# Delta rule: five second orientations of the inverse by TensorE transposes instead of second fp32 products

## The chip, the core and the metric

The kernel runs on one core of a Trainium2 chip, as one program. The metric is device microseconds of one execution; the runs are given as a median with the lowest and the highest. A core has TensorE for matrix products (results land in PSUM, eight banks of which this kernel names 4 "acc", 2 "mm" and 2 "tr"), VectorE, ScalarE and GpSimd for elementwise work, and SyncE, whose queue starts most DMAs. Every engine takes its own instructions in order; one that needs another engine's result waits on a semaphore.

## The reference, cut to what matters

A first stack of two layers works on 256 latent tokens (and 256 of context), a second stack of two layers on the 256 tokens alone. A layer of the second stack is FFN, mixer, FFN, each behind a norm. The mixer runs a gated delta rule with 8 heads beside a dilated attention with 12; both are merged by gates. The delta rule is worked out in chunks, and within a chunk a triangular system is solved:

```python
    m = jnp.where(strict, jnp.einsum('nbhid,nbhjd->nbhij', kb, kc) * decay, 0.0)
    a = m + jnp.eye(C, dtype=f32)
    u_c = lax.linalg.triangular_solve(a, vb, left_side=True, lower=True, unit_diagonal=True)
    w_c = lax.linalg.triangular_solve(a, kb * jnp.exp(gc)[..., None], left_side=True,
                                      lower=True, unit_diagonal=True)
    def step(state, xs):
        v_new = u_i - jnp.einsum('bhcd,bhde->bhce', w_i, state)
        o_i = (jnp.einsum('bhcd,bhde->bhce', q_i * jnp.exp(g_i)[..., None], state)
               + jnp.einsum('bhij,bhje->bhie', qk_i, v_new))
```

## The kernel before

All large products are done in two float32r parts of each factor, as three products of 128x128 by 256 columns (`mm3`: ah by w_hi, al by w_hi, ah by w_lo); the delta rule's small products are in fp32. Weight tiles come through `w_raw`, are split by ScalarE (`w_hi`) and VectorE (`w_lo`), up to three tiles ahead of their use.

The mixer is the class `Hybrid`. Its `inner` runs, one after the other, the products with `w_in` (23 groups of 256 columns after the first pairs), those of gate b, those with `w_b`, those of gate a, those with `w_a` and those with `w_o`. Beside them go "sides", generators that `pump` steps between two blocks of a product: `chains` (the heads of the delta rule), `convolve`, the dilated attention, the vectors of the conditions. Every instruction, whatever emits it, passes through `Engine.call`, so the profile shows line 75 for nearly all; the rows below are told apart by tiles.

`chains` holds up to four heads active (NB = 4). Each head is a generator, `delta`, whose steps end at a `yield`; a step is emitted when `Times`, a table of estimated costs, says that its inputs are ready. A head may start when its query, key and value have been convolved, and the places for queries and keys hold six heads. So the order of the work is fixed when the program is built, by the estimates, and on the chip each engine follows it in order.

`delta` treats two chunks of 128 tokens together (`for c in range(2)`), so a step has two products or a multiple. It first builds `MQ`, the masked products of the keys. Then it inverts 1 + M. `X` is the inverse and `XT` its transpose; both lie in one tile, `XX` (d_XX in the rows). `MT` is M's transpose within one level of blocks (`level`, made by GpSimd). Blocks of 8 come first, by squares, then four levels of 16, 32, 64 and 128 in the loop `for i in range(1, 5)`, in each a product lv by X into `t1` and one of t1 by XT, subtracted from XT. Each level needs X and XT, and before the change each of the pair is made by an fp32 product of its own into one half of a PSUM bank. After the inverse follow, each a step with one or two products: the new values (vb), the outputs and the state S (kd and MQ), the second chunk's (S with k and q, then S with XX, then MQ), a norm of the head's outputs (ScalarE's squares, GpSimd's power, VectorE's scaling), and two transposes of the output, after which the head is done.

Where the products of gate a end, a loop waits for the heads, with every step emitted at once whether or not its inputs are ready by the estimates:

```python
        while not chain.done:
            progress()
```

Only then do the products with `w_a` follow, which need all heads' outputs.

Of the kernel before, what the change touches and what calls it, by code (L numbers as in the profile page):

```python
# [28 lines left out]
class Times:  # L29
    """Estimates of the times at which the engines end what they have been given; by these the instructions of  # L30
    independent parts are put in order."""
# [33 lines left out]
class Engine:  # L65
    """An engine whose instructions' times are estimated as they are emitted."""
# [37 lines left out]
class Timed:  # L104
    """The engines, with estimates of their times."""
# [7 lines left out]
class Side:  # L113
    """Work emitted beside TensorE's products: without a rate, as it can go on; else up to rate steps per us of
    these, while what engine has been given ends within spare us."""
# [33 lines left out]
class Weights:  # L149
    """Weight tiles in the order of their use: loaded ahead, then split in two float32r parts."""  # L150
# [8 lines left out]
    def add(self, ap, offset, row, k, c):  # L159
        """A tile of k blocks of 128 rows by c columns, the first at offset, rows row apart."""  # L160
        self.plan.append((dview(ap, offset, [[row, 128], [128 * row, k], [1, c]]), k, c))
        return len(self.plan) - 1

    def up(self, wg, go, wu, uo, row, f0, f1, lead):
        """Pairs of the gate's and the other factor's columns; with lead, the tiles of the first two alternate."""
# [47 lines left out]
class Build:  # L213
    def __init__(self, nc, tc, I, out, es):
# [10 lines left out]
        # the residual stream, transposed; a second one (the context's); the modulated input in two parts  # L225
# [3 lines left out]
        # besides, for the products begun before a norm's statistics are known: its input * A, and B  # L229
# [9 lines left out]
    def ring(self, pool, shape, dtype, name, bufs):  # L239
        """A tile; its memory's last use counts in the times."""  # L240
        p, t = pool.tile(shape, dtype, name=name, bufs=bufs), self.times
        old = self.rings.setdefault(name, [])
        old.append(p)
        if len(old) > bufs:
            p0 = old.pop(0)
            t.note(t.read, p, max(t.when(x, p0) for x in (t.read, t.written)))
        return p

    def free(self, name, bufs):
        """The time at which the next of a ring's tiles is free."""  # L250
# [3 lines left out]
    def pipeline(self, n, stages, may=lambda i: True, begun=None):  # L254
        """The stages of n items, each when what it needs is done; later items' go in between. A stage: a function
        of the item, one that names its bank, and (s, m) if it may be at most m items before stage s."""
# [27 lines left out]
    def timed(self, gen):  # L284
        """Steps of gen, each when what the last one emitted will be done."""
# [13 lines left out]
    def bank(self, many):  # L299
        """A bank for a product's output; many: those for accumulation besides."""  # L300
# [15 lines left out]
    def rsqrt(self, dst, src, mul, add):  # L316
        """dst = (src * mul + add) ** -0.5"""
# [15 lines left out]
    def forced(self, f):  # L333
        """f(), in which nothing is waited for."""
# [4 lines left out]
    def run(self, gen):  # L339
        """gen yields where other work may go between its products."""  # L340
        for _ in gen:
            self.pump()

# [1 line left out]
    def load_consts(self):  # L345
        """What the first modulation needs."""
# [58 lines left out]
    def aln(self, i, j):  # L405
        """ALPHA * the norm's factors and shifts."""
# [9 lines left out]
    def ada_src(self, name):  # L416
        """name: (stack, layer, index)"""
# [5 lines left out]
    def ada_gen(self, pool, jobs):  # L423
        """The vectors of the conditions, on VectorE: weights times the condition's column, block after
        block; their sums over the partitions end with TensorE and wait in self.pending for that."""
# [44 lines left out]
    def partial(self, dst, t, acc):  # L470
        """Sums over the 32 partitions of a quarter: column 32 b + j of acc to partition j of the quarter, column b."""
# [3 lines left out]
    def reduce_one(self):  # L475
        """The sums over the quarters; those of columns 128 v + 32 c + j go to partition 32 c + j, column v."""
# [10 lines left out]
    def fill(self, n):  # L487
        """Work for TensorE while it would wait."""
# [14 lines left out]
    def mod_cols(self, shift, scale, g=None, b=None, mul=1.0):  # L503
        """Columns A, B of x * (1 + scale) + shift with x = n * g * mul + b."""
# [19 lines left out]
    def gemm_b(self, pairs, rhs, n, evac, ks=8, lead=False, tail=False, many=False, norm=None):  # L524
        """Outputs [128 columns, n tokens]; pairs: lists of the tiles (over k) of 256 columns.
        evac(first block, number of blocks, [128, blocks, 256]) for 256 tokens, evac(block, [128, 512]) for 512.
        lead: the first two pairs go together, block of k by block of k, as rhs comes; with a norm, begun before it,
        and evac has to add a column per block, its last argument.
        tail: the last pair's blocks come one by one. many: see bank()."""
# [35 lines left out]
    def gemm_early(self, pairs, norm, evac):  # L565
        """The first two pairs' products of a norm's input * A and of B; meanwhile the norm is done."""
# [47 lines left out]
    def gemm_a2(self, tiles, lhs, evac):  # L614
        """Outputs [128 tokens, 2 token tiles, 256 columns], in one bank; tiles over k."""
# [14 lines left out]
    def gemm_a(self, tiles, lhs, toks, evac, tags="acc", groups=1, middle=None):  # L630
        """Outputs [128 tokens, c columns] for each token tile; tiles over k. With groups > 1, all tiles for
        the first group of token tiles, then all for the next; middle: called amid the first group's."""
# [4 lines left out]
        for g in range(groups):  # L637
            ts = range(g * toks // groups, (g + 1) * toks // groups)
            kk = 0
            for n, ti in enumerate(tiles):  # L640
                if 0 < g == groups - 1:
                    # the tiles before this one are no longer needed
# [22 lines left out]
def norm_mem(tile):  # L665
    """Memory of a norm; tile(name, shape)"""
# [5 lines left out]
class Norm:  # L672
    """A norm over the features of h [128, 8, tokens], features in the partitions, for one or more streams
    (h, memory): the sums are gathered as blocks of 128 features come; then norm * A + B in two float32r parts.
    For a layer norm h is shifted by the mean of its first 256 features, which keeps the variance's differences
    small."""

    def __init__(self, b, kind, streams=None, slow=True):
        """slow: the blocks come slowly enough for GpSimd to add up the first ones."""
# [6 lines left out]
    def early(self, A, B):  # L686
        """The products with norm * A + B begin before the statistics are known."""
# [4 lines left out]
    def blocks(self, i, k, n):  # L692
        """Blocks k .. k + n - 1 of stream i have come."""
# [51 lines left out]
    def sums(self, i, keep=0):  # L745
        """The sums over the features, per token, but for the last blocks."""
# [13 lines left out]
    def stats(self, i=0):  # L760
        """Per token 1 / std, and -mean / std for a layer norm."""
# [13 lines left out]
    def spread(self, i):  # L775
        """The statistics in every partition, [128, tokens], in PSUM."""
# [6 lines left out]
    def finish(self):  # L783
        """The statistics of the first stream; while they come TensorE sums up vectors of the conditions."""
# [6 lines left out]
    def apply(self, hi, lo, A, B, i=0, each=None, middle=None):  # L791
        """hi, lo [128, 8, 256] of norm * A + B; for a layer norm h becomes the plain norm."""
# [62 lines left out]
def residual(b, gate, norm):  # L855
    """h += gate * product, block by block, and the next norm's sums."""
# [6 lines left out]
class Layer0:  # L863
    """Retention and FFN of the first layer: latents and context together (512 tokens)."""
# [3 lines left out]
    def __init__(self, b):  # L868
# [9 lines left out]
        for h in range(4):  # L878
# [3 lines left out]
            else:  # L882
                # they go together
# [39 lines left out]
    def residual(self, gates, norms):  # L923
        """evac(block, [128, 512]) of products."""
# [9 lines left out]
    def inputs(self, es):  # L934
        """The inputs, transposed and modulated by the first two vectors of the conditions, whose columns come 256
# [1307 lines left out]
```

## Time and profile before

| | |
|---|---|
| median of 3 runs | 2923.53 us (2921.91 to 2925.88) |
| span of the profiled execution, from its first instruction to its last | 2918.0 us |
| own time of the profiled execution beside its span | not given apart; the runs' median is 5.5 us above the span |
| TensorE busy | 2821.7 us, 97% |
| VectorE busy | 2106.7 us, 72% |
| ScalarE busy | 1308.9 us, 45% |
| GpSimd busy | 282.0 us, 10% |
| mean granted clock of TensorE | 0.978 |

Matmuls are pipelined and their ends are modelled, so the busy time of TensorE counts overlapping instructions' latency once and does not say how dense they are; the start of one and of the next do. "PEld" is TensorE's load of the stationary factor, shown apart. An fp32 product leaves two records in the trace, a transpose one. In a row of waits, the name behind the arrow is what came last. Times in timelines are us from the span's start.

### The profile page before, as it was taken

Reading aid. Unit: us, or ns where it says so; the run is one execution under the profiler, and the core shown is the slowest. Engines: PE = TensorE matmul, PEld = TensorE weight load, DVE = VectorE, ACT = ScalarE, POOL = GpSimd, SP = SyncE. Lnnn points to the kernel's source line nnn. Section 1 sums busy time; section 2 is a strip of 40 time slices with the busy share of each in tenths; the row PEclk is TensorE's granted clock in tenths of the full one; section 3 lists DMA queues with packets and bytes.
Section 4 is the critical chain, followed back from the end, with each engine's and each line's share of the span. In section 5 each row is a group of like instructions: output and inputs, shape, how many; then the busy total and the mean of one; then the engine's idle time right before and its main releaser. Section 6 shows DMA issues by size and latency. Waiting matters only on the chain.

```text
span 2918.0 us, 49485 instructions
## 1 busy us (share of the span) xinstructions
PE 2821.7 (97%) x19509; PEld 2591.5 (89%) x19509; DVE 2106.7 (72%) x3405; ACT 1308.9 (45%) x2229; POOL 282.0 (10%) x359
## 2 busy tenths in 40 slices
PE   8999998999999998998999999999999999999999
PEld 5878887888877788998999988999999998999999
DVE  6888887887877665787777777777565577666654
ACT  4433324322225444444445655444444466654543
POOL 0000002000010000001002223110010022130100
PEclk9999998999999998998999999999999999999999
DMA  6444441666654352875876523457556663224564
GB/s 236 146 145 136 142 149 55 220 224 218 233 181 141 99 136 94 265 257 173 276 259 201 148 84 113 142 184 228 185 169 184 186 179 116 80 76 151 166 185 132
DMA packets 432221, 488.36 MB, mean 167 GB/s; under 512 B 34650, under 2 KB 362300, under 8 KB 431988
## 3 DMA queue, kind: packets, MB, share of 16 engines
q1 hardware_dynamic: 430948, 484.59, 53.2%
q8 instruction: 153, 2.51, 0.4%
q10 hardware_dynamic: 1040, 0.60, 0.1%
q14 instruction: 80, 0.66, 0.1%
HBM read 484.07 MB, written 1.05 MB: 166 GB/s over the span
## 4 chain that ended last, share of the span: by engine, by line
PE 46%; DVE 4%; ACT 2%; issue 1%; POOL 1%; DMA 0%; DVEq 0%; ACTq 0%; POOLq 0%
PE ps_acc L75 24%; PE ps_mm L75 21%; DVE w_lo L75 1%; PE ps_tr L75 1%; ACT w_hi L75 1%; DVE n_t L75 1%; DVE al L75 0%; DVE n_a L75 0%; POOL d_t L75 0%; ACT n_a L75 0%; DVE d_XX L75 0%; DVE da_st L75 0%; POOL d_MT L75 0%; DVE ada_acc L75 0%; ACT d_t L75 0%
## 5 line engine op out<-in xcount | busy, mean ns | idle before, releaser
L75 DVE TENSOR_TENSOR w_lo<-w_raw,w_hi 128x1024 fp32r<-128x1024 f32 (+2 forms) x676 | 818.5, 1221 | 432.8 <-ACT w_hi L75 429.1
L75 ACT ACTIVATE w_hi<-w_raw 128x1024 fp32r<-128x1024 f32 (+2 forms) x686 | 700.6, 1030 | 505.5 <-PE ps_acc L75 226.2
L75 PE MATMUL ps_mm<-ah,w_hi 128*128 128x256 f32 (+2 forms) x2272 | 697.5, 307 | 15.2 <-ACT w_hi L75 7.7
L75 PE MATMUL ps_mm<-ah,w_lo 128*128 128x256 f32 (+2 forms) x2272 | 677.5, 298 | 2.2 <-DVE w_lo L75 2.2
L75 PE MATMUL ps_mm<-al,w_hi 128*128 128x256 f32 (+2 forms) x2272 | 678.6, 299 | 0.4
L75 PEld LDWEIGHTS ps_mm<-ah,w_hi 128*128 128x128 f32 (+1 forms) x2272 | 433.1, 191 | 39.8 <-issue 12.6
L75 PEld LDWEIGHTS ps_mm<-ah,w_lo 128*128 128x128 f32 (+1 forms) x2272 | 433.7, 191 | 16.9 <-DVE w_lo L75 3.2
L75 PEld LDWEIGHTS ps_mm<-al,w_hi 128*128 128x128 f32 (+1 forms) x2272 | 433.1, 191 | 12.9 <-DVE al L75 1.4
L75 PE MATMUL ps_acc<-ah,w_hi 128*128 128x256 f32 (+2 forms) x1456 | 436.9, 300 | 1.2 <-ACT ah L75 1.2
L75 PE MATMUL ps_acc<-al,w_hi 128*128 128x256 f32 (+2 forms) x1456 | 436.4, 300 | 0.4 <-DVE al L75 0.4
L75 PE MATMUL ps_acc<-ah,w_lo 128*128 128x256 f32 (+2 forms) x1456 | 435.5, 299 | 0.2 <-DVE w_lo L75 0.2
L75 DVE SCALAR_TENSOR_TENSOR ada_acc<-ada_w,cact,ada_acc 128x512 f32<-128x512 f32 x476 | 353.7, 757 | 14.9 <-DMA ada_w<-ada_w 10.2
L75 PEld LDWEIGHTS ps_acc<-ah,w_hi 128*128 128x128 f32 x1456 | 275.5, 189 | 11.3 <-ACT ah L75 1.6
L75 PEld LDWEIGHTS ps_acc<-ah,w_lo 128*128 128x128 f32 x1456 | 276.3, 190 | 10.4 <-DVE w_lo L75 0.7
L75 PEld LDWEIGHTS ps_acc<-al,w_hi 128*128 128x128 f32 x1456 | 275.6, 189 | 10.5 <-DVE al L75 0.7
L75 PE MATMUL ps_acc<-hh,w_hi 128*128 128x256 f32 (+1 forms) x800 | 237.0, 296 | 0.0
L75 PE MATMUL ps_acc<-hl,w_hi 128*128 128x256 f32 (+1 forms) x800 | 236.7, 296 | 0.0
L75 PE MATMUL ps_acc<-hh,w_lo 128*128 128x256 f32 (+1 forms) x800 | 236.6, 296 | 0.0
L75 POOL TENSOR_TENSOR n_a<-n_a 128x512 f32<-128x512 f32 (+1 forms) x28 | 40.4, 1443 | 1352.9 <-ACT n_a L75 1187.5
L75 PEld LDWEIGHTS ps_acc<-hh,w_lo 128*128 128x128 f32 x800 | 150.9, 189 | 4.4
L75 PEld LDWEIGHTS ps_acc<-hh,w_hi 128*128 128x128 f32 x800 | 150.9, 189 | 4.4
L75 PEld LDWEIGHTS ps_acc<-hl,w_hi 128*128 128x128 f32 x800 | 150.9, 189 | 4.4
(386 smaller groups left out, 4555.0 us busy)
## 6 DMA issues: line engine op xcount, KB each, us to landing
ada_w<-ada_w SPq DMA_DIRECT2D x448, 256.0 KB
w_raw<-w_in SPq DMA_DIRECT2D x132, 512.0 KB
w_raw<-ffn_w SPq DMA_DIRECT2D x128, 512.0 KB
w_raw<-ffn_wg SPq DMA_DIRECT2D x88, 512.0 KB
w_raw<-ffn_wu SPq DMA_DIRECT2D x88, 512.0 KB
w_raw<-ffn_wd SPq DMA_DIRECT2D x80, 512.0 KB
w_raw<-ret_w_in SPq DMA_DIRECT2D x48, 512.0 KB
w_raw<-na_w_qkv SPq DMA_DIRECT2D x24, 512.0 KB
```

Of the source, the lines that this page charges most:

```text
L75: r = f(*args, **kw)
```

## The change

Five times in a head, the second orientation of a matrix is no longer made by a second product in the same step. A new helper, `turned(dst, src)`, transposes both chunks of src on TensorE into a fresh bank and has ScalarE copy them to dst. It is used for MT (the square of M, from t1, where VectorE copied the second product's half before), for X after the square of the inverse, and for X after the first three levels of the loop. (The transposes into X at the start only move into the helper.) Each use is a step of its own, with a `yield` ahead of it. The subtraction in the loop works on XT alone, 256 columns in place of 512.

```diff
...
+        def turned(dst, src):
+
+            ps = bank()
+            for c in range(2):
+                tr(ps[:, cs[c]], src[:, c, :], ident)
+            act(dst, two(ps), AF.Copy)
+
         level(MT, 0)
         yield
         tt(out=XT, in0=eye, in1=MT, op=OP.subtract)
         yield
-        ps = bank()
-        for c in range(2):
-            tr(ps[:, cs[c]], MT[:, c, :], ident)
-        act(X, two(ps), AF.Copy)
+        turned(X, MT)
         yield
         ps = bank()
         for c in range(2):
             mm(ps[:, cs[c]], MT[:, c, :], X[:, c, :], start=True, stop=True)
-            mm(ps[:, 256 + 128 * c:384 + 128 * c], X[:, c, :], MT[:, c, :], start=True, stop=True)
         act(t1, two(ps), AF.Copy)
-        nc.vector.tensor_copy(MT, two(ps[:, 256:512]))
+        yield
+        turned(MT, t1)
         yield
...
         ps = bank()
         for c in range(2):
             mm(ps[:, cs[c]], X[:, c, :], XT[:, c, :], start=True, stop=True)
-            mm(ps[:, 256 + 128 * c:384 + 128 * c], XT[:, c, :], X[:, c, :], start=True, stop=True)
-        act(XX, both(ps), AF.Copy)
+        act(XT, two(ps), AF.Copy)
+        yield
+        turned(X, XT)
         yield
...
                 mm(ps[:, cs[c]], t1[:, c, :], XT[:, c, :], start=True, stop=True)
-                if i < 4:
-                    mm(ps[:, 256 + 128 * c:384 + 128 * c], XT[:, c, :], t1[:, c, :], start=True, stop=True)
+            tt(out=XT, in0=XT, in1=two(ps), op=OP.subtract)
+            yield
             if i < 4:
-                tt(out=XX, in0=XX, in1=both(ps), op=OP.subtract)
-            else:
-                tt(out=XT, in0=XT, in1=two(ps), op=OP.subtract)
-            yield
+                turned(X, XT)
+                yield
```

As the order of emission follows the estimates, it changes from the first head on. On ScalarE in the first layer, where the first head's square of M is copied, there stands now one copy more:

```order
 L75 ACTIVATE da_k<-ps_mm 128x512
 L75 ACTIVATE d_v<-n_t 128x256
+L75 ACTIVATE d_MT<-ps_acc 128x256
 L75 ACTIVATE w_hi<-w_raw 128x1024
 L75 ACTIVATE n_a<-n_a,da_st 128x128
```

The copy into MT has moved to ScalarE, between a value's convolution and a weight tile's split; VectorE's copy of the same matrix is gone from its own queue.

On TensorE in the second layer, where the last two heads end (tiles with their numbers; ident_76 by d_MT is the transposing of a head's output, d_S by d_XX the second chunk's new values, ps_mm rows are the products of gate a), the kernel before has:

```order
L75 MATMUL ps_acc_27018<-d_S_26883,d_XX_26284 128x128
L75 MATMUL ps_acc_27021<-ident_76,d_MT_26302 128x128 x2
L75 MATMUL ps_mm_26987<-ah_68,w_hi_26892 128x256
L75 MATMUL ps_mm_26987<-al_69,w_hi_26892 128x256
L75 MATMUL ps_mm_26987<-ah_68,w_lo_26893 128x256
```

At the corresponding place of the changed kernel (behind the last product of gate a; ps_mm_27344 is the first product with w_a) stands:

```order
L75 MATMUL ps_acc_27289<-d_XX_26679,d_MT_26787 128x128 x2
L75 MATMUL ps_acc_27295<-ident_76,d_MT_26563 128x128 x2
L75 MATMUL ps_acc_27299<-d_XX_26679,d_t1_26678 128x128 x2
L75 MATMUL ps_acc_27304<-d_vb_26785,d_XX_26679 128x128
L75 MATMUL ps_acc_27307<-d_t1_26678,d_kd_26786 128x128
L75 MATMUL ps_acc_27307<-d_t1_26678,d_MQ_26939 128x128
L75 MATMUL ps_acc_27312<-d_S_27303,d_k_26473 128x128
L75 MATMUL ps_acc_27312<-d_S_27303,d_q_26251 128x128
L75 MATMUL ps_acc_27317<-d_S_27303,d_XX_26679 128x128
L75 MATMUL ps_acc_27320<-d_t1_26678,d_MQ_26939 128x128
L75 MATMUL ps_acc_27332<-ident_76,d_MT_26787 128x128 x2
L75 MATMUL ps_mm_27344<-ah_68,w_hi_26972 128x256
```

Before, products of gate a stand between the last heads' steps, and 54 of them behind the last head's transposes; now the last head's steps stand next to each other, from the loop that waits for the heads, and the products with w_a directly behind.

## Rows read from the trace of the kernel before

**Rows 1.** The page's part 1: busy us, share of the span, instructions.
```profile
PE 2821.7 (97%) x19509; PEld 2591.5 (89%) x19509; DVE 2106.7 (72%) x3405; ACT 1308.9 (45%) x2229; POOL 282.0 (10%) x359
```

**Rows 2.** Each engine's busy us by windows: delta stage, first layer, then second.
```profile
1680.00:1720.00 40.00, 34.84 (x272) 32.33 (x271) 29.23 (x77) 23.73 (x57) 5.30 (x9) 0.96 0.24 68
...
2600.00:2640.00 40.00, 39.91 (x348) 39.53 (x347) 24.48 (x54) 17.69 (x50) 12.53 (x18) 1.00 0.28 80
```

**Rows 3.** TensorE's waits (us, times, longest): first layer; last row: second.
```profile
PE ps_acc L75 <- ACT d_t L75: 6.9, 4, 4.2
...
PE ps_acc L75 <- POOL d_t L75: 2.4, 2, 2.2
PE ps_acc L75 <- ACT d_XX L75: 2.0, 2, 1.3
PE ps_acc L75 <- DVE d_XX L75: 0.9, 2, 0.6
...
PE ps_acc L75 <- POOL d_t L75: 1.1, 2, 0.9
```

**Rows 4.** TensorE's timeline at four fp32 products: start, duration, operands.
```profile
1641.95 0.39 PE L75 MATMUL ps_acc<-d_XX,d_MT 128*128 128x128 f32 x2
...
1642.96 0.28 PE L75 MATMUL ps_mm<-al,w_hi 128*128 128x256 f32 x1
1643.08 0.29 PE L75 MATMUL ps_mm<-ah,w_lo 128*128 128x256 f32 x1
```

**Rows 5.** The same timeline at two transposes.
```profile
1636.56 0.38 PE L75 MATMUL ps_acc<-ident,d_MT 128*128 128x128 f32 x2
...
1636.90 0.28 PE L75 MATMUL ps_mm<-al,w_hi 128*128 128x256 f32 x1
```

**Rows 6.** Tile view of XX: count, ns min/median/max, first, last start.
```profile
L75 PE MATMUL ps_acc<-d_t,d_XX x192: 275/275/421, 1670.0 to 2634.8; 128*128 128x128 f32 x192
...
L75 PE MATMUL ps_acc<-d_XX x128: 270/275/348, 1652.5 to 2620.1; 128*128 128x128 f32 x128
L75 DVE TENSOR_TENSOR d_XX<-d_XX,ps_acc x80: 404/678/690, 1649.3 to 2638.4; 128x512 f32<-128x512 f32 x48, 128x256 f32<-128x256 f32 x32
...
L75 PE MATMUL ps_acc<-d_MT,d_XX x64: 275/275/275, 1642.2 to 2614.7; 128*128 128x128 f32 x64
```

**Rows 7.** Timeline of weight loads, the second layer's last head.
```profile
2636.45 0.52 PEld L75 LDWEIGHTS ps_acc<-d_XX,d_MT 128*128 128x128 f32 x4
...
2637.69 0.52 PEld L75 LDWEIGHTS ps_acc<-d_XX,d_t 128*128 128x128 f32 x4 [0.28 <-ACT d_t L75]
...
2638.92 0.30 PEld L75 LDWEIGHTS ps_acc<-d_vb,d_XX 128*128 128x128 f32 x2
...
2639.84 0.31 PEld L75 LDWEIGHTS ps_acc<-d_t,d_MQ 128*128 128x128 f32 x2
```

**Rows 8.** ScalarE's timeline at the same place.
```profile
2637.26 0.38 ACT L75 ACTIVATE d_t<-ps_acc 128x256 f32<-128x256 f32 x1 [1.04 <-PE ps_acc L75]
```

**Rows 9.** VectorE's timeline, the same head's last steps.
```profile
2638.44 0.42 DVE L75 TENSOR_TENSOR d_XX<-d_XX,ps_acc 128x256 f32<-128x256 f32 x1 [0.45 <-PE ps_acc L75]
...
2652.39 0.28 DVE L75 TENSOR_TENSOR d_MT<-d_MT,ps_acc 128x128 f32<-128x128 f32 x1
...
2656.77 0.47 DVE L75 TENSOR_SCALAR d_MT<-d_MT,d_st 128x128 f32<-128x128 f32 x2
```

**Rows 10.** GpSimd's timeline, the same head's norm.
```profile
2654.23 0.95 POOL L75 TENSOR_TENSOR d_st<-d_st,mhalf 128x2 f32<-128x2 f32 x1
```

**Rows 11.** TensorE's busy us and granted clock by windows, first layer.
```profile
1685.00:1690.00 5.00, 1.61 (x14) 1.00 0.01 2
1690.00:1695.00 5.00, 4.19 (x21) 0.66 0.37 110
```

**Rows 12.** TensorE's timeline: the product that ends the first window's wait.
```profile
1690.81 0.49 PE L75 MATMUL ps_acc<-d_k 128*128 128x128 f32 x2 [4.21 <-ACT d_t L75]
```

More of the change, by code (lines that the diff above doesn't have):

```diff
@@ L1974, in delta @@
         yield
-        def both(ps):
-            return ps.rearrange("p (a c n) -> p a c n", a=2, c=2)
         ps = bank()
```

## The prediction

> **What bounds the kernel now.** I read the page first. TensorE is busy for 97% of the span, VectorE for 72%, ScalarE for 45% [rows 1]. A busy TensorE is not always a useful one, so the windows over the two mixers come next: in the second layer's delta stage 39.91 of 40 us are busy, and the worst window of the first layer's still has 34.84 [rows 2]. The waits of TensorE in these stages say what the rest is. In the first layer 6.9 us end with ScalarE's copies into t1, 2.4 with GpSimd's scaled mask, 2.0 and 0.9 with copies and subtractions into XX, 12.2 us together; in the second the longest such group is 1.1 us [rows 3]. So TensorE's own instruction stream is the limit in this part of the program: the delta rule is laid between the large products, its hand-offs hide behind them, and a microsecond of TensorE work removed there is a microsecond off the end, as long as products remain to hide the hand-offs.
>
> **What the swap saves.** One fp32 product of 128x128 takes two TensorE passes: four of them, the first at 1641.95, run until the next product's pace is reached, (1642.96 - 0.12 - 1641.95) / 4 = 0.2225 us each, 0.12 us being the pitch of the large products [rows 4]. Two transposes run from 1636.56 to 1636.90 - 0.12, so 0.11 us each [rows 5]. Each swap is worth 0.1125 us of TensorE. The counts come from the tile view, at two records for a product [rows 6]: 192 / 2 = 96 products t1 by XX in the loop, 64 / 2 = 32 with MT as the stationary side, and half of the 128 / 2 = 64 squares of X, which is 32. All of these 160 become transposes: 160 x 0.1125 = 18.0 us saved, 9.0 us in each layer.
>
> The Trainium skill (FP8 and Floating Point Precision, TensorE Precision Notes) counts four passes of the array for a true fp32 product. Were a transpose a single pass of the four, the ratio would be 4 to 1, the saving 160 x 0.167 = 26.7 us instead of 18.0, and the forecast below would come out 8.7 us lower. The rows show 2 to 1, and the rows decide; I give it no chance of its own.
>
> **What it adds off TensorE.** A product that came out of the same bank as its twin now has to wait for that twin's copy, be transposed and be copied again: 5 more steps in each head's chain, 35 in place of 30, 80 over 16 heads. Engine time is no problem by itself. ScalarE gets five more 256-column copies a head at 0.38 us [rows 8], 1.9 us a head and 30 us over both layers at most (its one 512-column copy gets shorter), on an engine busy for 23.7 of 40 us [rows 2]. VectorE's three subtractions fall from 0.68 us [rows 6] to 0.42 [rows 9]. None of this is on TensorE's path while products cover it.
>
> **The cover runs out.** Here the order decides. Before, the last transposes of a layer's last head stand 78 (first layer) and 54 (second layer) product rows ahead of the end of the gate's products, 9 and 6 us at 0.12 us each. With five steps more per head, and head 4 starting only when head 0 has left its buffers, the heads are not done when the gate's products end. The loop ahead of the products with w_a then emits all that is left at once, with nothing in between: 36 TensorE instructions in the first layer, 47 in the second, counted in the order of the change. In this tail TensorE waits for each hand-off.
>
> The price of a hand-off is read where the last head ran almost alone, from the load of one step's weights to that of the next [rows 7]. A pair of products and ScalarE's copy: 2636.45 to 2637.69, 1.24 us, the copy starting at 2637.26 [rows 8]. A pair and VectorE's subtraction: to 2638.92, 1.23 us. A single product and a copy of 128 columns: to 2639.84, 0.92 us. A turn (two transposes and a copy) is in no row as such; I take the pair's step less 2 x 0.11, 1.02 us. The head's last stretch is a product (0.58 us to its result), the norm from VectorE's addition at 2652.39 [rows 9] to GpSimd's power ending at 2654.23 + 0.95 [rows 10], then 0.47 us of scaling [rows 9] and 0.05 us for each of two hand-offs: 3.9 us before the last transposes can go.
>
> Second layer: the last head has still to go through 9 pair steps (11.1), 3 turns (3.1), 2 single ones (1.8) and the last stretch (3.9), with 0.4 of transposes and a product ahead and 0.2 behind: 20.6 us. In the same rows stand 33 products and 14 transposes, 33 x 0.22 + 14 x 0.11 = 8.9 us of work that has to be done anyway. Idle: 11.7 us. First layer: 6 pair steps (7.4), 1 turn (1.0), 2 single ones (1.8), the last stretch (3.9) and 0.7 at the ends: 14.8 us, less 26 products and 10 transposes, 6.9 us. Idle: 7.9 us. Together 19.6 us. From below I bound this by 16 us, if the second head in the tail and the engines' queues overlap a sixth better than the steps alone; from above by 24 us, if a weight split of about 1 us stands ahead of a copy on ScalarE or VectorE a few times.
>
> **Two smaller terms.** Hand-offs that do stand between products cost TensorE (12.2 + 1.1) / 480 = 0.03 us a step before [rows 3]; 80 more steps add 2 us. Bounds: nothing, or a stall as that at 1690.81, where TensorE stood 4.21 us [rows 12], once more. Then the clock. That stall left 1.61 us busy in five, and the next five ran at a mean granted clock of 0.66, a stretch at 1.2 GHz in place of 2.4, 0.34 x 5 = 1.7 us lost [rows 11]. Each tail ends in a head alone, whose pair steps keep TensorE at work for under half the time, and in 3 us of nothing. I expect one such stretch at least in each: 3.4 us from below if it falls, 6.8 if two do; I take 4.
>
> **Sum.** -18.0 + 19.6 + 2 + 4 = +7.6 us. The profiled execution's span is 2918.0 us, which becomes 2925.6. The profile gives no other time of that execution; the median of the runs lies 5.5 us above the span, so I carry the difference over: 2923.5 + 7.6 = 2931.1 us, 0.26% slower. A measurement of this kernel can tell about 0.2%, 5.8 us.
>
> **Rivals.**
> (a) The clock holds in the tails. For it: a tail is not empty, two heads overlap in most of it. Against it: [rows 11]. It gives 2923.5 - 18.0 + 19.6 + 2 = 2927.1, no change to be told.
> (b) Faster: the new interleaving loses the first layer's own stalls, the 12.2 us of [rows 3], with them the 1.7 us of slow clock behind the longest, and adds no new ones, so that the 2 us fall away too: 2931.1 - 15.9 = 2915.2. VectorE's shorter subtractions and the spread of the heads over more products speak for it; against it, the longest ended with a copy on ScalarE [rows 12], which gets more of these. It decides from 13.4 us on, nearly all of the 15.9, since the forecast has to fall from 7.6 us above the old time to 5.8 below it.
> (c) ScalarE comes late in the middle: two more stalls of 4.2 us, each with its 1.7 us of clock: 2931.1 + 11.8 = 2942.9. For it: in-order copies, 30 us more of them. Against: 23.7 of 40 us busy.
> (d) Transposes lower the clock among the products. One slow stretch for each of 16 heads, 16 x 1.7 = 27 us: 2958. Against it: beside the transposes at 1636.56 the products keep their 0.12 us pitch [rows 4, 5]. The Trainium skill (TensorE: Matmul & The Clock Gate, Part 4: PE-mode transpose) says that a transpose does not count as a busy TensorE in the way that a product does; by that rule more transposes mean more slow stretches, and the trace bears it out nowhere that products stand on both sides.
>
> **Chances.** The forecast 0.50, (a) 0.27, (b) 0.08, (c) 0.12, (d) 0.03. The forecast's own range is 2926 to 2938. A third of it lies within 0.2% of 2923.5, so: slower 0.34 + 0.15 = 0.49, the same 0.16 + 0.27 = 0.43, faster 0.08. The range for 8 in 10 runs from 2921 (the tails at their lower bound, clock unharmed) to 2942, leaving out most of (b) and (d) and half of (c).
>
> **What would show it.** In the changed profile: TensorE's delta instructions as 160 fewer products, 0.11 us each for the transposes; waits of TensorE for XX, t1 and S copies of some 8 and 12 us in the last 15 to 21 us ahead of w_a's products, where before there were none; the granted clock at a half there or right behind; layers otherwise as before. Wrong are: the steps, if the tails measure under 14 us idle in all; the clock term, if it stays at 1.00 through both; the whole, if the waits ahead of the tails change by more than 6 us either way.

## The result, and the profile after

| | before | after |
|---|---|---|
| median | 2922.72 us (2920.82 to 2925.88, 4 runs) | 2939.6 us (2934.06 to 2943.99, 4 runs) |
| ratio | | 1.0054 [1.0041, 1.0066] |
| span of the profiled execution | 2918.0 us | 2932.3 us |
| mean granted clock of TensorE | 0.978 | 0.973 |

The changed kernel is 16.9 us slower by the medians, 12 to 19 by the interval of the ratio. The forecast said 7.6 us slower, in a range of 2921 to 2942: the sign and the range hold, but the forecast size is less than half of the measured one.

The page's part 1 of the changed kernel, which answers to [rows 1]:

```profile
PE 2820.6 (96%) x19349; PEld 2585.8 (88%) x19349; DVE 2095.8 (71%) x3389; ACT 1326.5 (45%) x2309; POOL 293.2 (10%) x359
```

160 TensorE instructions are gone, two for each product becoming one for each transpose; ScalarE has 80 more. Rows of the tile view of XX show 128 of the 160 transposes (the other 32 turn t1), beside [rows 6] (count, ns min/median/max, first and last start):

```profile
L75 PE MATMUL ps_acc<-ident,d_XX x128: 270/272/477, 1658.9 to 2664.6; 128*128 128x128 f32 x128
L75 ACT ACTIVATE d_XX<-ps_acc x112: 357/383/407, 1596.8 to 2664.9; 128x256 f32<-128x256 f32 x112
L75 DVE TENSOR_TENSOR d_XX<-d_XX,ps_acc x80: 402/415/423, 1647.3 to 2667.4; 128x256 f32<-128x256 f32 x80
```

The windows that answer to [rows 2], one of the first and one of the second layer's delta stage (busy us of PE, PEld, DVE, ACT and POOL, then TensorE's clock), and the longest waits of TensorE in the first layer, which answer to [rows 3]:

```profile
1680.00:1720.00 40.00, 35.12 (x261) 32.73 (x260) 28.25 (x75) 23.70 (x59) 5.71 (x10) 0.91 0.30 86
2600.00:2640.00 40.00, 39.17 (x334) 38.39 (x333) 24.70 (x53) 23.68 (x68) 19.98 (x24) 1.00 0.28 87
```

```profile
PE ps_acc L75 <- DVE d_MT L75: 5.3, 5, 2.4
PE ps_acc L75 <- DVE d_MQ L75: 3.9, 2, 2.6
...
PE ps_acc L75 <- ACT d_t L75: 1.0, 3, 0.4
```

The copies into t1 (d_t in the rows) on which TensorE waited for 6.9 us now hold it for 1.0. VectorE's MQ has come in their place, and its work on a head's outputs, which lie in MT's tile by then; of the 5.3 us on these, 2.9 belong to the end of the layer, the tail below. The second layer's window at 2600 is full as before, so the loss is not here.

To place the time I matched the large products (those with w_hi or w_lo, the same in every kernel) of two traces by number. Between the 6000th, ahead of the first mixer of the second stack, and the 12000th, between the two mixers, the changed kernel gains 1.2 us on the kernel before; from there to the last it loses 17.4. These are called the layers' lags below, -1.2 and 17.4. Ahead of the 6000th, where the programs are alike, traces lie -1.9 to 10.2 us from before's, so a lag places a difference better than a median does. Each lag is that of one traced execution. Where other runs repeat a layer's instructions, one by one, the second layer's lag comes again within 0.1 us (17.3), and layers left as before give lags of 0.3 us at most; but the changed first layer gives -1.2, 3.3 and -0.2 in three traces, so a first-layer lag is known to some 4 us only.

The second layer's lag has two places. The first is in the middle of the stage. TensorE's busy time and granted clock (the column behind POOL's) by windows, changed kernel, then the kernel before:

```profile
2585.00:2590.00 5.00, 1.74 (x13) 1.36 (x12) 3.57 (x7) 2.19 (x7) 0.30 (x1) 0.94 0.26 91
2590.00:2595.00 5.00, 2.95 (x10) 2.48 (x11) 3.92 (x7) 2.97 (x8) 3.86 (x3) 0.50 0.73 205
2595.00:2600.00 5.00, 5.00 (x27) 5.00 (x26) 3.11 (x7) 1.26 (x4) 0.89 (x1) 0.54 0.39 115
```

```profile
2585.00:2590.00 5.00, 4.14 (x34) 3.85 (x33) 1.99 (x3) 1.55 (x6) 4.00 (x6) 1.00 0.23 79
2590.00:2595.00 5.00, 4.71 (x42) 4.50 (x41) 3.85 (x11) 3.17 (x12) 2.27 (x5) 1.00 0.17 36
```

The timeline there (start, duration, engine; in brackets the idle time before and what ended it) tells why:

```profile
2583.88 2.94 DVE L75 SCALAR_TENSOR_TENSOR n_t<-cv_x,cwT,n_t 128x255 f32<-128x255 f32 x6
...
2587.34 0.35 DVE L75 SCALAR_TENSOR_TENSOR d_S<-ps_acc,negc,d_vb 128x128 f32<-128x128 f32 x1
2587.78 0.37 ACT L75 ACTIVATE d_MT<-ps_acc,egc 128x128 f32<-128x128 f32 x1 [5.53 <-DVE d_S L75]
...
2590.38 0.37 ACT L75 ACTIVATE d_XX<-ps_acc 128x256 f32<-128x256 f32 x1
...
2590.80 1.22 PE L75 MATMUL ps_acc<-d_XX,d_MT 128*128 128x128 f32 x4 [2.29 <-ACT d_XX L75]
```

Read from the bottom: TensorE waits for a copy into XX. ScalarE makes it late because it had stood idle for 5.53 us, the instruction at the head of its queue waiting for VectorE's d_S, and what had piled up behind that instruction (a head's squares, two weight splits) goes ahead of the copy. VectorE had six convolution instructions in a row, 2.94 us, ahead of that d_S. They are the 64th to 69th of the layer's 72, those of late heads. TensorE's waits from 2582 to 2597, the copy and two more from the same queues:

```profile
PE ps_acc L75 <- ACT d_XX L75: 2.3, 1, 2.3
PE ps_mm L75 <- DVE sb L75: 1.8, 1, 1.8
PE ps_acc L75 <- POOL d_t L75: 1.2, 1, 1.2
```

The second place is the tail. The weight loads there, to be read against [rows 7], by windows after that:

```profile
2663.20 0.52 PEld L75 LDWEIGHTS ps_acc<-d_XX,d_t 128*128 128x128 f32 x4 [0.50 <-ACT d_t L75]
2664.47 0.20 PEld L75 LDWEIGHTS ps_acc<-ident,d_XX 128*128 128x128 f32 x2 [0.75 <-DVE d_XX L75]
2665.44 0.52 PEld L75 LDWEIGHTS ps_acc<-d_XX,d_MT 128*128 128x128 f32 x4 [0.77 <-POOL d_st L75]
...
2666.69 0.52 PEld L75 LDWEIGHTS ps_acc<-d_XX,d_t 128*128 128x128 f32 x4 [0.25 <-ACT d_t L75]
...
2672.02 0.50 PEld L75 LDWEIGHTS ps_acc<-d_t,d_MQ 128*128 128x128 f32 x2 [0.66 <-ACT d_t L75]
2675.75 0.38 PEld L75 LDWEIGHTS ps_acc<-ident,d_MT 128*128 128x128 f32 x2 [3.24 <-DVE d_MT L75]
```

```profile
2665.00:2670.00 5.00, 3.16 (x17) 2.23 (x17) 1.50 (x5) 1.27 (x4) 0.69 (x1) 1.00 0.00 0
2670.00:2675.00 5.00, 2.00 (x8) 1.23 (x8) 1.38 (x6) 2.01 (x9) 0.50 (x2) 0.63 0.01 2
2675.00:2680.00 5.00, 4.24 (x20) 4.23 (x21) 3.53 (x8) 1.61 (x3) 0.38 (x1) 0.50 0.00 0
2680.00:2685.00 5.00, 5.00 (x38) 5.00 (x37) 1.71 (x2) 1.06 (x1) 0.00 (x0) 0.84 0.38 116
```

A pair with VectorE's subtraction takes 2664.47 - 2663.20 = 1.27 us, a turn 0.97, a pair with ScalarE's copy 1.25, the norm at the end 2675.75 - 2672.02 = 3.73 us. No large product stands between. The two ends of the tail are the last product of gate a and the first with w_a:

```profile
2654.20 0.28 PE L75 MATMUL ps_mm<-ah,w_lo 128*128 128x256 f32 x1
...
2676.10 0.56 PE L75 MATMUL ps_mm<-ah,w_hi 128*128 128x256 f32 x1
```

With the pitch of 0.12 us [rows 4] that is 21.8 us. The first layer's tail reads in the same way, 15.2 us; behind its ends, the windows around the first product with w_a:

```profile
1867.29 0.29 PE L75 MATMUL ps_mm<-ah,w_lo 128*128 128x256 f32 x1
...
1882.63 0.56 PE L75 MATMUL ps_mm<-ah,w_hi 128*128 128x256 f32 x1
```

```profile
1880.00:1885.00 5.00, 3.40 (x15) 3.06 (x16) 3.25 (x12) 2.78 (x8) 0.88 (x2) 0.50 0.00 0
1885.00:1890.00 5.00, 5.00 (x39) 5.00 (x39) 3.47 (x4) 1.06 (x1) 0.00 (x0) 0.87 0.49 161
```

The lag tells the same story. In the second layer it is -6.7 us at the last product of gate a, 15.1 at the first with w_a and 17.6 some 40 products later.

### The profile page after: what moved, and what is told of

It reads as the page before. It is cut to its first block, busy times and chain, and to the rows that moved or that the text cites. A ratio compares the mean times of both kernels' runs of the same rounds, so it can differ in the third digit from the quotient of the medians.

```text
span 2932.3 us, 49254 instructions
## 1 busy us (share of the span) xinstructions
PE 2820.6 (96%) x19349; PEld 2585.8 (88%) x19349; DVE 2095.8 (71%) x3389; ACT 1326.5 (45%) x2309; POOL 293.2 (10%) x359
## 4 chain that ended last, share of the span: by engine, by line
PE 45%; DVE 5%; ACT 3%; issue 1%; POOL 0%; ACTq 0%; DVEq 0%
PE ps_acc L75 23%; PE ps_mm L75 21%; DVE w_lo L75 1%; PE ps_tr L75 1%; ACT w_hi L75 1%; DVE n_t L75 1%; DVE al L75 1%; DVE n_a L75 0%; ACT n_a L75 0%; DVE d_XX L75 0%; DVE d_MT L75 0%; ACT d_MT L75 0%; ACT d_t L75 0%; DVE da_st L75 0%; POOL d_t L75 0%
## 5 line engine op out<-in xcount | busy, mean ns | idle before, releaser
L75 PE MATMUL ps_mm<-ah,w_hi 128*128 128x256 f32 (+2 forms) x2272 | 704.7, 310 | 17.7 <-ACT w_hi L75 7.7
```

Source lines behind the costliest of these rows:

```text
L75: r = f(*args, **kw)
```

## The experiments

Two theories were put to the chip. A: the swap itself saves what it should, and what is lost is lost where a head has no large products beside it (the tails), later also behind a blocked queue in the middle. B (called the rival where it has another form): the 80 added hand-offs cost TensorE wherever they stand. Runs 1 to 4 are compared with a median of 2923.88 us of the kernel before, 5 to 8 with 2924.6, 9 to 12 with 2924.59. Where a turn is undone, the second product and its copy are back, as before.

**1. The loop's turns alone** (96 swaps). MT and the square keep their second product:

```diff
+            mm(ps[:, 256 + 128 * c:384 + 128 * c], X[:, c, :], MT[:, c, :], start=True, stop=True)
         act(t1, two(ps), AF.Copy)
-        yield
-        turned(MT, t1)
+        nc.vector.tensor_copy(MT, two(ps[:, 256:512]))
...
+            mm(ps[:, 256 + 128 * c:384 + 128 * c], XT[:, c, :], X[:, c, :], start=True, stop=True)
-        act(XT, two(ps), AF.Copy)
-        yield
-        turned(X, XT)
+        act(XX, both(ps), AF.Copy)
```

> Only the three turns in the loop are taken over; MT and the square keep their second products. 96 of the 160 swaps: 10.8 us of TensorE saved, 48 of the 80 added steps. In this kernel's order the first layer's heads end ahead of the end of gate a's products, and in the second the last head has 4 steps left there. Theory A (the uncovered tail decides): -10.8 us, +4 us idle in the second layer's short tail, +3 us of stalls and clock: about 4 us faster than before, 2919. Theory B (every added step costs the same, 16 us / 80 = 0.2 us net of its saving): 48 steps give +10 us, 2933.

Measured: 2915.32 us, ratio 0.9973 [0.9962, 0.9983]. Lags -9.3 and 1.4 us. 48 more steps, and faster than before: B falls. A had 2919. The first layer gains more than the 5.4 us of work saved in it, and so it does in runs 8 and 12 (-8.7 and -7.8), so its order also loses less to waits.

**2. MT's and the square's turns alone** (64 swaps): the loop keeps its second product and its subtraction of 512 columns.

```diff
+                if i < 4:
+                    mm(ps[:, 256 + 128 * c:384 + 128 * c], XT[:, c, :], t1[:, c, :], start=True, stop=True)
-            tt(out=XT, in0=XT, in1=two(ps), op=OP.subtract)
-            yield
-            if i < 4:
-                turned(X, XT)
-                yield
```

> Only the two turns ahead of the loop (MT and the square) are taken over; the loop keeps its second products. 64 swaps, 7.2 us saved, 32 added steps, but in this kernel's order the last head still has 12 steps left at the end of gate a's products in the first layer and 15 in the second. Theory A: -7.2 us, some 16 us idle in the two tails, +5 us of clock and stalls: about 14 us slower than before, 2937. Theory B: 32 steps at 0.2 us give +6 us, 2929.

Measured: 2945.08 us, ratio 1.0078 [1.0063, 1.0093]; lags 9.7 and 13.9. A third fewer steps than in run 1 and 30 us more time: the number of steps doesn't set the time. A had 2937, so it misses by 8 us, though on the right side. The order's tails are long, 16.6 and 25.4 us between gate a's last product and the first with w_a. TensorE's waits in the second layer:

```profile
PE ps_acc L75 <- ACT d_t L75: 5.1, 6, 1.6
PE ps_acc L75 <- DVE d_XX L75: 4.8, 5, 3.4
...
PE ps_acc L75 <- DVE d_MT L75: 2.9, 1, 2.9
```

Of these, 7.4 us stand in the tail (3.5 of the first row, 1.0 of the second and the third whole). The longest, 3.4 us for XX, stands far ahead of it, at 2494.

**3. All turns, for heads 2 to 5 only** (80 swaps; every turn under `2 <= h < 6`). The last heads are as before, so there is no tail.

> All five turns, but for heads 2 to 5 alone; heads 0, 1, 6 and 7 are as before. 80 swaps, 9.0 us saved, 40 added steps; in this kernel's order all heads end ahead of the end of gate a's products in both layers. Theory A: -9.0 us, no tail, +2 us of stalls: about 7 us faster, 2916. Theory B: 40 steps at 0.2 us give +8 us, 2931.

Measured: 2919.04 us, 0.998 [0.9971, 0.9989]; lags -1.2 and -1.9. On A's side, but of 9.0 us of TensorE work saved only 3 to 5 arrive. There is no tail, so the rest goes to waits in the middle, which are not taken apart here.

**4. All turns, first layer only** (`self.l == 0`), with its tail.

> The whole change in the first layer of the second stack, the second layer as before. Theory A with the trace of the changed kernel: the first layer's tail (15 us) is about paid by its saving, so -1 to +2 us, 2923, and nearly all of the 16 us is the second layer's. Theory B: half of the 16 us, +8 us, 2931.

Measured: 2922.01 us, 0.9999 [0.999, 1.0008]; lags 3.3 and 0.1. No difference that can be told, as A has it. (The trace is that of the slowest of ten executions, 2929.31 us.)

**5. Stale turns.** The steps and waits of before; each second product becomes a transpose of a matrix at hand, so that X and MT hold other values than the method needs.

```diff
-            mm(ps[:, 256 + 128 * c:384 + 128 * c], XT[:, c, :], X[:, c, :], start=True, stop=True)
+            tr(ps[:, 256 + 128 * c:384 + 128 * c], X[:, c, :], ident)
```

> The kernel before, with each of the five second products replaced, in the same step and bank, by transposes of a matrix that is at hand there (so X and MT hold other values than they should; the steps, their number and their waits stay as before). It has the changed kernel's TensorE work without its 80 added steps. In this order the second layer's heads end 18 product rows ahead of the end of gate a's products, the first layer's last head has 12 steps left. Theory A: the 160 swaps are worth 18.0 us, so the second layer alone is 9 us faster than before, the first gives back some 8 in its tail: 2923.9 - 18 + 10 = 2916. Rival (transposes lower the clock, or TensorE is not the bound): the second layer gains under 4 us, 2925 or more.

Measured: 2903.99 us, 0.9937 [0.9917, 0.9956], 20.6 us below before by the medians, and 12 below A's 2916; lags -4.4 (this layer's order still has a tail, of 12 steps) and -11.9. The saved work is real: the second layer, without a tail, gains more than A's 9 and far more than the rival's 4. What gave the 3 us beyond the 9 is not shown. The mean clock, 0.976 to 0.978 over four executions, is that of before (0.974 to 0.978 in the executions beside them).

**6. A filled tail.** The loop that waits for the heads also issues products that nobody reads.

```diff
         while not chain.done:
             progress()
+            for _ in range(6 if self.alone else 2):
+                nc.tensor.matmul(spare[:, 0:256], mh[:, 0, 0:128], mh[:, 1, 0:256], start=True, stop=True)
```

> The changed kernel, with products that nobody reads emitted in the loop that waits for the heads, 2 behind each step and 6 where only one head is left, so that TensorE is not idle there. Theory A with a clock term: the granted clock stays at 1.00 through and behind both tails, and the time falls from the changed kernel's 2939.6 by what the slow stretches at 1879 and 2671 cost, 4 to 6 us: 2935. Rival (the slow clock falls in idle time and costs nothing, or the clock falls all the same): 2939 to 2943.

Measured: 2941.56 us, 1.0065 [1.005, 1.008]; lags 4.5 and 15.8. The time is that of the rival, 2939 to 2943, but the clock did what A said. Windows of its second tail, and the weight loads at its end:

```profile
2680.00:2685.00 5.00, 4.82 (x42) 4.62 (x40) 1.49 (x6) 2.10 (x9) 0.59 (x2) 1.00 0.00 0
2685.00:2690.00 5.00, 4.33 (x36) 4.27 (x37) 3.53 (x8) 1.53 (x3) 0.29 (x1) 1.00 0.02 5
```

```profile
2685.67 0.33 PEld L75 LDWEIGHTS ps_acc<-ident,d_MT 128*128 128x128 f32 x2 [1.05 <-DVE d_MT L75]
2685.87 2.71 PEld L75 LDWEIGHTS ps_mm<-ah 128*128 128x128 f32 x22
2688.51 0.19 PEld L75 LDWEIGHTS ps_mm<-ah,w_hi 128*128 128x128 f32 x1
```

The clock stays at 1.00 through the tails, and the 2.5 us that the changed kernel's second layer loses behind its tail are not lost. But the time between the last product of gate a and the first with w_a is 4.0 and 3.9 us longer. Of that, 2.5 and 2.6 us are fillers that the loop still issued behind the last head's last transposes, as the rows show for the second layer; the rest, 1.5 and 1.3 us, is the chain's own products queuing behind fillers. So the run shows that this filling doesn't pay. It doesn't show that the clock is free: the hand-offs remain the larger part, but fillers that ended with the last head could, as an estimate from these numbers, win up to about 1 us a layer.

**7. All turns, second layer only** (`self.l == 1`).

> The whole change in the second layer of the second stack, the first as before. Theory A with the trace of the changed kernel: the second layer costs 17 us, 2923.9 + 16 = 2940, with a tail of 22 us behind gate a's products and a stall of VectorE's evacuations some 80 us ahead of it. Rival (the stall is an accident of one execution or of the first layer's order): 2930.

Measured: 2940.39 us, 1.0061 [1.0048, 1.0075]; lags -0.2 and 17.3. The whole loss is the second layer's. The stall in its middle comes again, 12 us later in the span:

```profile
2600.00:2605.00 5.00, 2.14 (x11) 1.97 (x12) 3.13 (x5) 4.20 (x11) 2.30 (x3) 0.72 0.17 43
2605.00:2610.00 5.00, 3.75 (x17) 3.28 (x15) 2.91 (x7) 1.84 (x6) 1.85 (x2) 0.50 0.87 270
```

**8. A mix without a tail:** the loop's turns in both layers, the square's in the second (112 swaps). In its order all heads end ahead of gate a's last product.

> The loop's three turns in both layers, and the square's in the second alone: 96 + 16 = 112 swaps, 12.6 us saved; in this order both layers' heads end ahead of the end of gate a's products, without a tail. Theory A: first layer as in the kernel with the loop's turns (-10 us), the second -7.2 us with 2 us of stalls: 2923.9 - 15 = 2909. Theory B (a cost for each step, 64 steps): 2937.

Measured: 2924.82 us, 1.0004 [0.9996, 1.0013]; lags -8.7 and 11.5. Here A, as it stood, falls: no tail, and the second layer loses all the same. The timeline shows the longest wait:

```profile
2564.46 0.31 ACT L75 ACTIVATE d_t<-d_MT 128x128 f32<-128x128 f32 x1 [2.96 <-DVE d_MT L75]
...
2565.31 0.36 ACT L75 ACTIVATE ah<-ps_tr 64x256 fp32r<-64x256 f32 x1
...
2566.91 0.80 ACT L75 ACTIVATE n_a<-n_a,da_st 128x128 f32<-128x128 f32 x2 [1.24 <-DVE da_st L75]
2567.36 1.09 PE L75 MATMUL ps_tr<-ident,n_a 128*128 128x128 f32 x3 [6.11 <-ACT n_a L75]
```

The dilated attention's transposes wait 6.11 us for a scaling that stands on ScalarE behind a delta step's squares and copies, which wait for VectorE. Two waits for copies into XX, 5.4 us together, stand apart from it. So the theory has to be wider: a step that is not ready blocks the queue of VectorE or ScalarE for whatever is queued behind it. The order, which rests on estimates, decides where that meets TensorE.

**9. Convolutions split, second layer.** The changed kernel with all 160 swaps; the three convolution instructions of a head's query, key or value are three steps, so that six no longer stand in a row.

```diff
                 stt(t[:, s:], x[:, :256 - s], w[k], t[:, s:], op0=OP.mult, op1=OP.add)
+                if self.l == 1 and k:
+                    yield
```

> The changed kernel, all 160 swaps; in the second layer the three convolution instructions of a head on VectorE are three steps in place of one, so that six of them no longer stand in a row ahead of a delta step. In the order this also lets the late heads begin earlier, and the second layer's last head ends 18 product rows ahead of the end of gate a's products: no tail there. Theory A (the second layer's 17 us were its tail and the stall behind six convolutions in a row, and the saved TensorE work is real): that layer comes to 6 to 9 us below before, the first stays near 1 us below, 2914 to 2917 us. Rival (80 more hand-offs find other blocked queues in the middle, as with the mix of 112 swaps, 11 us): 2933 to 2940 us.

Measured: 2921.11 us, 0.9985 [0.9976, 0.9994], 18 us below the changed kernel; lags -0.2 and -3.1, so the second layer comes 20.5 us forward. The stall at that place and the layer's tail are gone. Windows where the changed kernel had its stall, and the one behind the last heads' end:

```profile
2585.00:2590.00 5.00, 4.48 (x37) 4.24 (x37) 3.59 (x8) 1.56 (x4) 4.25 (x6) 1.00 0.30 105
2590.00:2595.00 5.00, 5.00 (x43) 4.89 (x42) 1.46 (x3) 4.13 (x13) 1.79 (x4) 1.00 0.08 25
...
2660.00:2700.00 40.00, 39.75 (x335) 39.57 (x335) 28.54 (x40) 19.58 (x27) 0.10 (x1) 1.00 0.54 173
```

In the changed kernel 33.04 of those last 40 us are busy, at a clock of 0.87. A shorter stall, 2.8 us of waiting for a copy into XX, stands elsewhere in the stage. The lags take the 20.5 us apart: at gate a's last product run 9 has -2.9 us and no delta work left, the changed kernel -6.7 us and 8.9 us of work left (the prediction's count of its tail). So some 5 us come from the middle and 15 from the tail and the slow clock behind it. The time misses A's 2914 to 2917; the next run bears on that.

**10. The kernel before with the same split.**

> The kernel before, with its second products, and the same splitting of the second layer's convolutions. Theory A (before, nothing in that layer waits for the convolutions): 2921 to 2926 us, as before. Rival (the splitting itself makes the layer faster, and the changed kernel's gain would be the splitting's): 2912 to 2917 us.

Measured: 2931.5 us, 1.0023 [1.0014, 1.0031]; lags -0.3 and 6.7. Neither expectation had this: splitting alone costs. Its longest wait of TensorE in that stage is again one of the dilated attention, for a copy behind an instruction that waits for VectorE, here one of a convolution:

```profile
PE ps_tr L75 <- ACT n_a L75: 3.9, 1, 3.9
```

With the split on both sides, the swap takes the second layer from 6.7 to -3.1 us, 9.8 us, and the medians from 2931.5 to 2921.11. That is close to the 9.0 us a layer that the pitches gave.

**11. Convolutions split in both layers** (`if k:` in run 9's edit); 5 steps are left in the first layer's tail.

> The changed kernel with convolutions split in both layers; the order leaves 5 steps of 30 in the first layer's tail, 5 us of hand-offs, and none in the second's. Theory A: first layer 5 to 8 us below before, second 6 to 9 below, 2907 to 2912 us. Rival (other blocked queues in the middle): 2922 to 2935 us.

Measured: 2911.64 us, 0.9955 [0.9942, 0.9967]; lags -7.0 and -2.8. A's total, 2907 to 2912, and its 5 to 8 us for the first layer hold; the second layer gave 2.8 us where A had 6 to 9, so the total holds partly by luck.

**12. The loop's turns in the first layer, all turns and the split in the second** (run 1's edit under `self.l == 0`, with run 9's).

> First layer with the loop's turns alone (as the run that took 10 us off it), second layer with all turns and split convolutions; no tail in either, 128 swaps, 14.4 us of TensorE work less. Theory A: 10 us from the first and 6 to 9 from the second layer, 2905 to 2908 us, at or below the kernel of stale turns, 2904, which keeps its first layer's tail. Rival (the second layer's gain is eaten by other stalls): 2914 to 2925 us.

Measured: 2911.88 us, 0.9959 [0.9947, 0.9972]; lags -7.8 and -3.2. Between the two expectations: the first layer gives nearly what it gave in run 1, the second, the same instructions as in runs 9 and 11, again 3 us in place of 6 to 9. Runs 11 and 12 beat before and after alike, and can't be told from each other.

## Why the prediction was half right

- **What the swap saves: right.** 18.0 us was the term. Runs 9 and 10 show 9.8 for one layer against 9.0. Run 5 has 20.6 by the medians and 16.3 by its lags, with a tail still in it; that is more than the term, and its order differs too. The prediction's two passes for a product are two records in the trace, not a count of passes: 0.2225 us are 3.7 times the 0.06 us of 128 columns at the large products' pitch [rows 4]. That is near the four passes of the Trainium skill (FP8 and Floating Point Precision, TensorE Precision Notes). The prediction's estimate of 26.7 us from them, 13.4 a layer, failed on its other half, a transpose of one pass: at 0.11 us [rows 5] it takes nearly two by the same measure.
- **The tails: right, a little small.** 14.8 and 20.6 us were forecast (the terms given for the second add up to 20.5), 15.2 and 21.8 came. Less the work of 6.9 and 8.9 us in them, 8.3 + 12.9 = 21.2 us stood idle, against 19.6. The steps had their price: 1.25, 1.27, 0.97 and 3.73 us against 1.24, 1.23, 1.02 and 3.9.
- **The clock: right.** Behind the first product with w_a, half speed lasts 3.9 us and then a sixth of five is missing: 0.5 x 3.9 + 0.16 x 5 = 2.8 us; the lag there grows by 2.5. In the first layer the same sum from 1882.63 is 0.5 x 2.4 + 0.13 x 5 = 1.9 us. 4.7 us against 4. What is slow ahead of that falls in time in which TensorE mostly waits; the steps there kept their price.
- **The hand-offs in the middle: wrong.** This is the step that failed: "80 more steps add 2 us". An average of 0.03 us a step, taken from the kernel before, was spread over steps that cost nothing or several us. What is left of the lags tells the size. First layer: -1.2 + 9.0 - 8.3 - 1.9 = -2.4 us, which can't be told from nothing where the same instructions give lags from -1.2 to 3.3. Second: 17.4 + 9.0 - 12.9 - 2.8 = 10.7 us, where 1 was set. Most of that is the stall at 2585. Its three windows show 50 TensorE records, 6 us of work at 0.12 us each, so some 9 of 15 us are lost: 5.3 us of waits, and clocks of 0.94, 0.50 and 0.54.
- **The average itself was read too low.** The second layer's delta stage begins at 2383; its rows in [rows 2, 3] are from 2600 and from 2540 on. Ahead of that the kernel before has a wait nearly as long as the first layer's longest, 4.2 us, with a slow clock behind it:

```profile
PE ps_acc L75 <- ACT d_t L75: 3.5, 1, 3.5
```

```profile
2470.00:2475.00 5.00, 1.51 (x14) 1.32 (x13) 2.72 (x5) 3.38 (x9) 2.25 (x4) 1.00 0.00 0
2475.00:2480.00 5.00, 5.00 (x31) 4.55 (x31) 4.69 (x18) 2.64 (x7) 0.74 (x1) 0.66 0.36 105
```

The whole second stage has 6.7 us of such waits in place of 1.1. That makes the average 0.04 us and the term 3 us, so it doesn't mend the forecast; it shows that costs came in single stalls before the change too.
- **The range and the sign of being wrong.** 2939.6 lies in the range because its upper end took in half of (c); the sum had no term of that size, so that is luck in part. The sign set for the whole, waits ahead of the tails changed by more than 6 us, did not show: they go from 12.2 to 9.9 us in the first layer and from 6.7 to 12.4 in the second. It counted waits and left out the slow clock behind them.
- **The rivals.** (c), ScalarE late in the middle, came true once where it was priced twice, at some 9 us against 5.9 for one. Its cause was looked for in the wrong place: the 30 us of added copies play no part in the rows; ScalarE was late because the head of its queue waited for VectorE, which was behind with six convolutions. (a) gave a holding clock; it did not hold. (b) needed nearly all of 15.9 us; the first layer's waits fell by 2.3 us and changed their kind, from copies into t1 to others. (d) is refuted by run 5: with 160 transposes among the products the clock is that of before. The Trainium skill (TensorE: Matmul & The Clock Gate, Part 4: PE-mode transpose) says that a transpose doesn't count as busy in the same way; for transposes that stand among products, run 5 shows no cost of that.
- **What is shown and what is argued.** That the second layer's loss goes with its order is shown (runs 7, 9, 10). Run 9 removes stall and tail together; its lags put 15 us to the tail and the clock behind it, as the sum above does (15.7), but only 5 to the middle, where the sum has 10.7: run 9's order has waits of its own there. That the six convolutions made the stall is read from one trace, and the stall comes again in run 7; no run removes them and leaves the rest of the order alone. The split was chosen for them; that it also ends the tail, because the late heads start earlier, comes from the order, not from a measured chain. Why splitting costs 6.7 us by itself is shown only as far as the one wait of 3.9 us.

## What to carry to other kernels

Where small dependent steps hide between large products, saving engine time by adding steps pays only as far as the cover reaches: count how many steps of the last chain come behind the last product, at the price of a hand-off, before counting what each step saves. Price a hand-off by the chain in which it runs alone, and don't carry an average wait over to steps that are put elsewhere: one instruction that isn't ready at the head of an in-order queue blocks everything behind it (5.53 us on ScalarE here). If a swap loses, look at the order before giving it up: here the same 160 swaps lost 17 us or won 13, by whether three convolution instructions were one step or three in each layer.

## What the runs showed of the hardware

- TensorE at 3.16 us busy of five between hand-offs still ran at 1.00; the clock fell in the window behind it, with 2.00 us busy, and stayed at the lower level well into the dense products that follow (0.50, then 0.84).
- Products that nobody reads held the clock at 1.00 through both tails (run 6), and the time did not fall: they stand in the same queue as the chain that they were to help, and made the tails 4 us longer, 2.5 of these behind the chain's end.
- The changed kernel's four executions run the same instructions and lie 9.9 us apart; the mean granted clock goes with it, 0.973 at 2934.06 us and 0.969 at 2942.1 and 2943.99.
